# A hybrid decoder layer on one core: the output projection of the first token half with channels on the partitions

## The chip, the cores and the metric

The kernel runs on one core of a Trainium2 chip. The metric is device time in microseconds (us). Before the change the median of three runs is 2372.8 us (2372.53 to 2372.96).

## The reference, cut to what matters

One layer over 1024 tokens and 2048 channels in float32: an RMS norm, one wide input projection, two recurrent mixers (mLSTM and HGRN2), and then the tail, which is all that the change touches:

```python
y = jnp.concatenate([y_a, y_b], axis=-1)                       # (1, 1024, 2048)
h = h + jnp.einsum('bsc,cd->bsd', y, w_out)                    # output projection, residual
e = jnp.einsum('bsr,rd->bsd', p, w_pe)                         # 256 -> 2048
gate = jax.nn.sigmoid(jnp.einsum('bsd,de->bse', rmsnorm(h, pe_norm_w), w_pg))
h = h + gate * e
out = rmsnorm(h, final_norm_w)                                 # over the channels of a token
```

## The kernel before, in words

The tokens are worked in two halves of 512 (`half` 0 and 1). First both halves go through the input projection and the mixers; the mixers leave `y` with channels on the 128 partitions and tokens along the row, in device memory (`y_dram`, 16 pieces a half). Then the tail runs for half 0 and for half 1.

Every float32 operand of a large matmul is split into a high and a low part (`split`, lines 119 and 120: a cast on ScalarE, a subtraction on VectorE), and `mm3` (lines 253 to 255) makes three matmuls of each product. Weights come as pieces of 128x1024, loaded and split three pieces ahead (`next_piece`, `load_piece`).

The tail of a half, before: the sixteen `y` pieces are loaded (`yr`, three staging buffers, line 692) and split into `ys`, tiles of the pool `upool`. `upool` has 17 buffers under one tag, and all of these use it: the inputs `u` of the projections, `ys`, and the results `h2`, two blocks of 128x512 in one tile. Four column blocks `cb` of the output projection follow. In each, the stationary operand is a 128-token slice of `ys` and the moving one is 512 weight columns, so that a result `ps[t]` has 128 tokens on the partitions and 512 channels in the row. VectorE adds the residual (`ht`, line 720), ScalarE squares it into a sum per token (line 722), `h` goes to memory, and TensorE transposes the four 128x128 blocks of each of four channel groups (`pht`, line 729), because the next matmul contracts over the channels. From the transposed block come the two parts of `hn` (lines 732, 733). In the gate's four blocks, ScalarE takes the sigmoid straight from the result with the norm of the token as a per-partition scale (line 785), VectorE multiplies by `pe`, adds `h` and the final norm's weight (lines 786, 792, 797). After the last block the norm `r3` of each token is a scalar per partition: eight tiles of a half are scaled on ScalarE (line 809), eight on VectorE (lines 805, 807), and all are written out (line 810).

The order of the work is not written by hand: a list scheduler plays the program on a timing model and fixes the order on each engine, earlier instructions of the program first among those that are ready; buffers of one tag are handed to tiles by the pool. The engines then keep that order on the chip. Work of different stages is interleaved: the first column blocks of half 0's output projection run while the last HGRN2 unit of half 1 is still at work. The pool `tl`, which holds `pp`, `hn` and the small tiles of the tail, lies where the mixers' tiles were.

Lines that the steps touch:

```python
692  nc.sync.dma_start(out=yr, in_=y_dram[half][k])
720  nc.vector.tensor_tensor(out=ht, in0=ps[t], in1=xr, op=ALU.add)
729  nc.tensor.transpose(pt[:, t * P:(t + 1) * P], hts[t][:, j * P:(j + 1) * P], ident)
788  h2t = upool.tile([P, 2, HT], F32, tag="u", name=f"h2_{half}_{cb}_{t}")
809  nc.scalar.activation(out=ho, in_=ho, func=AF.Copy, scale=r3)
```

Of the kernel before, what the change touches and what calls it, by code (L numbers as in the profile page):

```python
# [16 lines left out]
F32 = mybir.dt.float32  # L17
F32R = mybir.dt.float32r
BF16 = mybir.dt.bfloat16
U32 = mybir.dt.uint32  # L20
AF = mybir.ActivationFunctionType
ALU = mybir.AluOpType
AX = mybir.AxisListType

P = 128
S = 1024
D = 2048
KT = D // P
HT = 512
NC = HT // P  # L30
# [8 lines left out]
HOLD = 2  # L39
LATE = [f"bg1_3_{pc}" for pc in (1, 3, 5, 7)]  # L40

V_NORM, V_PEN, V_MLN, V_HGN, V_LB, V_CW, V_CB, V_END = 0, 16, 32, 40, 48, 64, 96, 104


@with_exitstack
def hybrid_layer(ctx: ExitStack, tc, x, xT, pT, w_blk, w_v0, w_vw, w_out, w_pg, w_pe, vec, gb, fnw,
                 ident_in, causal_in, lmask_in, out):
    nc = tc.nc
# [3 lines left out]
    upool = ctx.enter_context(tc.tile_pool(name="upool", bufs=17))  # L52
# [13 lines left out]
    def psj(name):  # L66
        return pj.tile([P, 512], F32, tag="pj", name=name)
# [5 lines left out]
    vec_sb = const.tile([P, V_END], F32, name="vec_sb")  # L73
# [3 lines left out]
    ident = const.tile([P, P], F32, name="ident")  # L77
# [5 lines left out]
    ones = const.tile([P, P], F32, name="ones")  # L83
# [27 lines left out]
    state_c = [None] * 4  # L111
    state_s = [None] * 8

    y_dram = [[tc.dram_tile([P, HT], F32, name=f"y_{h}_{k}") for k in range(KT)] for h in range(2)]
    h_dram = [tc.dram_tile([P, D], F32, name=f"h_{t}") for t in range(8)]


    def split(dst_hi, dst_lo, src):
        nc.scalar.copy(out=dst_hi, in_=src)  # L119
        nc.vector.tensor_tensor(out=dst_lo, in0=src, in1=dst_hi.bitcast(F32), op=ALU.subtract)  # L120
# [9 lines left out]
    for half in range(2):  # L130
        for b in range(32):
# [4 lines left out]
            for pc in range(4):  # L136
                if b - 4 in WIDE:
                    continue
                src = w_v0 if b == 2 else w_blk[b]
# [33 lines left out]
    def load_piece(name):  # L173

        while len(w_tiles) < len(w_order) and (len(w_tiles) < AHEAD or w_order[len(w_tiles) - AHEAD][0] != name):
            next_piece()
        return dict(w_tiles[-AHEAD - 4:])[name]
# [494 lines left out]
    for half in range(2):  # L672
# [5 lines left out]
        if half == 1:  # L678
            mlctx.close()
            xh = ctx.enter_context(tc.tile_pool(name="xh", bufs=4, side="right", reuse_waits="tile"))  # L680
# [4 lines left out]


    tl = ctx.enter_context(tc.tile_pool(name="tl", bufs=1, reuse_waits="tile"))
    for half in range(2):
        ys = []
        for k in range(KT):  # L690
# [5 lines left out]
        pp = tl.tile([P, 2, 2 * HT], F32R, tag="pp", bufs=1, name=f"pp{half}")  # L696
        for kk in range(2):
            pr_ = stage.tile([P, HT], F32, tag="xs", name=f"praw{half}_{kk}")
            nc.sync.dma_start(out=pr_, in_=pT[:, kk, half * HT:(half + 1) * HT])
            split(pp[:, 0, kk * HT:(kk + 1) * HT], pp[:, 1, kk * HT:(kk + 1) * HT], pr_)  # L700
        hns = [None] * KT
        ss = small.tile([P, NC, 4], F32, tag="ssx", name=f"ss2_{half}")
        for cb in range(4):
            ps = [psj(f"po{half}_{cb}_{t}") for t in range(NC)]
            for pc in range(8):
                hl = load_piece(f"o{half}_{cb}_{pc}")
                for kk in range(2):
                    k = pc * 2 + kk
                    for t in range(NC):
                        ts = slice(t * P, (t + 1) * P)  # L710
                        sl = slice(kk * 512, (kk + 1) * 512)
                        mm3(ps[t], ys[k][:, 0, ts], ys[k][:, 1, ts], hl[:, 0, sl], hl[:, 1, sl], k == 0, k == KT - 1)
            hts = []
            for t in range(NC):
                tt = half * NC + t
                cs = slice(cb * 512, (cb + 1) * 512)
                xr = xh.tile([P, 512], F32, tag="xr", name=f"xr{half}_{cb}_{t}")
                nc.sync.dma_start(out=xr, in_=x[tt * P:(tt + 1) * P, cs])
                ht = xh.tile([P, 512], F32, tag="ht", name=f"ht{half}_{cb}_{t}")
# [5 lines left out]
            for j in range(4):  # L725
                k = cb * 4 + j
                pt = psm(f"pht{half}_{k}")
                for t in range(NC):
                    nc.tensor.transpose(pt[:, t * P:(t + 1) * P], hts[t][:, j * P:(j + 1) * P], ident)
                hn = tl.tile([P, 2, HT], F32R, tag="hn2", bufs=16, name=f"hnt{half}_{k}")  # L730
                pw = vec_sb[:, V_PEN + k:V_PEN + k + 1]
                nc.scalar.activation(out=hn[:, 0], in_=pt, func=AF.Copy, scale=pw)
                nc.vector.scalar_tensor_tensor(out=hn[:, 1], in0=pt, scalar=pw, in1=hn[:, 0].bitcast(F32),
                                               op0=ALU.mult, op1=ALU.subtract)
# [6 lines left out]
        h2 = [[None] * 4 for t in range(NC)]  # L741
# [78 lines left out]
def _layout(inp):  # L820
    f = np.float32
    x = np.ascontiguousarray(np.asarray(inp["x"])[0])
    w = np.asarray(inp["w_in"])[0]
    cols = []
    for h in range(4):
        cols.append([(h * 128, 128), (512 + h * 128, 128)])
        cols.append([(2048 + h * 256, 256)])
        cols.append([(1024 + h * 256, 256)])
        cols.append([(3072 + h * 256, 256)])
    for p in range(4):  # L830
        q, fg, i, g = 4104 + p * 256, 5128 + p * 256, 6152 + p * 256, 7176 + p * 256
        cols.append([(i, 256)])
        cols.append([(q, 128), (fg, 128)])
        cols.append([(q + 128, 128), (fg + 128, 128)])
        cols.append([(g, 256)])
    v0 = np.empty((P, KT, 264), f)
    v0[:, :, 0:256] = w[:, 1024:1280].reshape(KT, P, 256).transpose(1, 0, 2)
    v0[:, :, 256:264] = w[:, 4096:4104].reshape(KT, P, 8).transpose(1, 0, 2)
    blk = np.empty((32, P, KT, 256), f)
    for b, cs in enumerate(cols):  # L840
        o = 0
        for c, n in cs:
            blk[b, :, :, o:o + n] = w[:, c:c + n].reshape(KT, P, n).transpose(1, 0, 2)
            o += n
    vw = np.empty((3, P, KT, 512), f)
    for i, b in enumerate(WIDE):
        vw[i, :, :, 0:256] = blk[b]
        vw[i, :, :, 256:512] = blk[b + 4]

    def blocks(m, kt):  # L850
        return np.ascontiguousarray(np.asarray(m)[0].reshape(kt, P, 4, 512).transpose(2, 1, 0, 3))

    vec = np.empty((P, V_END), f)
    vec[:, V_NORM:V_NORM + 16] = np.asarray(inp["norm_w"])[0].reshape(16, P).T
    vec[:, V_PEN:V_PEN + 16] = np.asarray(inp["pe_norm_w"])[0].reshape(16, P).T
    vec[:, V_MLN:V_MLN + 8] = np.asarray(inp["ml_norm_w"])[0].reshape(8, P).T
    vec[:, V_HGN:V_HGN + 8] = np.asarray(inp["hg_norm_w"])[0].reshape(8, P).T
    vec[:, V_LB:V_LB + 16] = np.asarray(inp["hg_lb"]).reshape(16, P).T
    vec[:, V_CW:V_CW + 32] = np.asarray(inp["conv_w"])[0].reshape(4, 8, P).transpose(2, 1, 0).reshape(P, 32)
    vec[:, V_CB:V_CB + 8] = np.asarray(inp["conv_b"])[0].reshape(8, P).T  # L860
    gb = np.stack([np.asarray(inp["ml_b_i"])[0], np.asarray(inp["ml_b_f"])[0]], axis=1)

    ident = np.eye(P, dtype=f)
    jj, tt = np.meshgrid(np.arange(P), np.arange(P), indexing="ij")
    causal = np.where(jj <= tt, 0.0, -BIG).astype(f)
    lm = np.zeros((P, NMASK, 64), np.uint32)
    j = np.arange(P)[:, None]
    c = np.arange(64)
    lm[:, 0] = j == 2 * c
    lm[:, 1] = j == c // 2 * 4  # L870
    lm[:, 2] = j == c // 2 * 4 + 1
    for li, s in enumerate(LEVELS):
        t = (c // s) * 2 * s + s + c % s
        lm[:, 3 + li] = (j // (2 * s) == t // (2 * s)) & ((j // s) % 2 == 0)
    return {
        "x": x, "xT": np.ascontiguousarray(x.T),
        "pT": np.ascontiguousarray(np.asarray(inp["p"])[0, 0].T.reshape(2, P, S).transpose(1, 0, 2)),
        "w_blk": blk, "w_v0": v0, "w_vw": vw, "w_out": blocks(inp["w_out"], KT), "w_pg": blocks(inp["w_pg"], KT),
        "w_pe": blocks(inp["w_pe"], 2), "vec": vec, "gb": np.ascontiguousarray(gb),
        "fnw": np.ascontiguousarray(np.asarray(inp["final_norm_w"]).reshape(1, D)),  # L880
        "ident": ident, "causal": causal, "lmask": lm,
    }
# [16 lines left out]
```

## Time and profile before

| | |
|---|---|
| median of 3 runs | 2372.8 us (2372.53 to 2372.96) |
| the profiled execution's own time | 2372.51 us |
| its span in the trace | 2370.5 us |
| TensorE (PE) busy | 2355.8 us, 99% of the span |
| VectorE (DVE) busy | 1170.9 us, 49% |
| ScalarE (ACT) busy | 765.8 us, 32% |
| granted TensorE clock, mean | 0.999 |

Busy time is the time in which at least one instruction of the engine runs. Matmuls overlap in the pipeline: one of 512 columns is shown 0.39 us long, but the next starts 0.227 us after it, so starts, not lengths, give its cost. "PE" is the matmul, "PEld" the weight load, "SPq" the queue that issues most DMAs.

### The profile page before, as it was taken

The numbers are of one execution on the slowest core, as the hardware profiler recorded it, in microseconds if no ns is written. First come the engines' busy times: TensorE is split into PE (matmuls) and PEld (weight loads), VectorE is DVE, ScalarE is ACT, GpSimd is POOL, SyncE is SP. The second block draws the span as 40 slices with busy tenths as digits, with TensorE's granted clock in tenths as the row PEclk, the third lists the DMA queues.
The fourth block names the chain that finished last, engine by engine and source line by source line (L and its number), as shares of the span: only waits on it lengthen the run. The fifth ranks groups of instructions, "written<-read, shape, count | busy, mean of one in ns | idle before, by whom it ended". The sixth has DMA issues, their size and how long they took to land.

```text
span 2370.5 us, 28577 instructions
## 1 busy us (share of the span) xinstructions
PE 2355.8 (99%) x11548; PEld 1984.1 (84%) x11548; DVE 1170.9 (49%) x1657; ACT 765.8 (32%) x1211; POOL 66.3 (3%) x96
## 2 busy tenths in 40 slices
PE   9999999999999999999999999999999999999998
PEld 7898888888888898988888888888888888888887
DVE  6655254265556857343534563675433444333336
ACT  6433232222222434232322222241423334332235
POOL 0000000000000000000000000000000000000000
PEclk9999999999999999999999999999999999999999
DMA  8433332322222423333333222343444456444436
GB/s 322 140 99 107 97 101 87 107 82 88 83 96 90 151 72 116 92 113 98 99 115 98 80 82 88 89 147 125 138 125 133 133 157 221 140 153 134 120 117 217
DMA packets 93452, 287.42 MB, mean 121 GB/s; under 512 B 10872, under 2 KB 11640, under 8 KB 93320
## 3 DMA queue, kind: packets, MB, share of 16 engines
q1 hardware_dynamic: 88200, 268.82, 36.5%
q0 software_dynamic: 5120, 16.78, 1.8%
q8 instruction: 90, 1.47, 0.3%
q14 instruction: 42, 0.34, 0.0%
HBM read 260.36 MB, written 25.20 MB: 120 GB/s over the span
## 4 chain that ended last, share of the span: by engine, by line
PE 99%; DMA 0%; DVE 0%; SPq 0%; ACT 0%; issue 0%; ACTq 0%; POOLq 0%
PE pj L254 15%; PE pj L253 15%; PE pj L255 15%; PE pt L253 5%; PE pt L255 5%; PE pt L254 5%; PE po L253 5%; PE pg L253 5%; PE po L255 5%; PE pg L254 5%; PE po L254 5%; PE pg L255 5%; PE pl L594 2%; PE pe L255 1%; PE pe L254 1%; PE pe L253 1%
## 5 line engine op out<-in xcount | busy, mean ns | idle before, releaser
L253 PE MATMUL pj<-u,hl 128*128 128x512 f32 x1536 | 603.5, 394 | 5.3 <-ACT hl L119 5.3
L254 PE MATMUL pj<-u,hl 128*128 128x512 f32 x1536 | 602.4, 392 | 0.1
L255 PE MATMUL pj<-u,hl 128*128 128x512 f32 x1536 | 601.2, 392 | 0.0
L120 DVE TENSOR_TENSOR hl<-raw,hl 128x1024 fp32r<-128x1024 f32 (+2 forms) x259 | 313.7, 1212 | 449.2 <-ACT hl L119 448.4
L119 ACT CAST hl<-raw 128x1024 fp32r<-128x1024 f32 (+2 forms) x259 | 269.4, 1040 | 819.8 <-PE pj L255 554.1
L253 PEld LDWEIGHTS pj<-u,hl 128*128 128x128 f32 x1536 | 288.8, 188 | 64.8 <-ACT hl L119 5.3
L254 PEld LDWEIGHTS pj<-u,hl 128*128 128x128 f32 x1536 | 289.1, 188 | 59.9 <-DVE u L241 0.9
L255 PEld LDWEIGHTS pj<-u,hl 128*128 128x128 f32 x1536 | 289.0, 188 | 59.6 <-issue 0.2
L254 PE MATMUL pt<-hl,u 128*128 128x512 f32 (+2 forms) x640 | 223.7, 350 | 0.0
L253 PE MATMUL pt<-hl,u 128*128 128x512 f32 (+2 forms) x640 | 222.9, 349 | 0.5 <-DVE raw L385 0.5
L255 PE MATMUL pt<-hl,u 128*128 128x512 f32 (+2 forms) x640 | 221.9, 348 | 0.0
L253 PE MATMUL po<-hl_o,ys 128*128 128x512 f32 x512 | 200.5, 393 | 0.0
L254 PE MATMUL po<-hl_o,ys 128*128 128x512 f32 x512 | 200.0, 391 | 0.0
L255 PE MATMUL po<-hl_o,ys 128*128 128x512 f32 x512 | 199.4, 390 | 0.0
L253 PE MATMUL pg<-hl_g,hnt 128*128 128x512 f32 x448 | 174.9, 390 | 0.0
L254 PE MATMUL pg<-hl_g,hnt 128*128 128x512 f32 x448 | 174.5, 390 | 0.0
L255 PE MATMUL pg<-hl_g,hnt 128*128 128x512 f32 x448 | 174.3, 389 | 0.0
L120 DVE TENSOR_TENSOR hl_o<-raw_o,hl_o 128x1024 fp32r<-128x1024 f32 x64 | 78.4, 1225 | 153.9 <-ACT hl_o L119 153.9
L120 DVE TENSOR_TENSOR hl_g<-raw_g,hl_g 128x1024 fp32r<-128x1024 f32 x56 | 68.6, 1225 | 167.4 <-ACT hl_g L119 167.4
L253 PEld LDWEIGHTS pt<-hl,u 128*128 128x128 f32 x640 | 120.6, 189 | 15.7 <-issue 0.8
L254 PEld LDWEIGHTS pt<-hl,u 128*128 128x128 f32 x640 | 120.8, 189 | 14.9 <-issue 0.2
L255 PEld LDWEIGHTS pt<-hl,u 128*128 128x128 f32 x640 | 120.5, 189 | 15.0 <-issue 0.2
(263 smaller groups left out, 2638.4 us busy)
## 6 DMA issues: line engine op xcount, KB each, us to landing
raw<-in_w_blk_dram SPq DMA_DIRECT2D x199, 512.0 KB, 3.9
raw_o<-in_w_out_dram SPq DMA_DIRECT2D x64, 512.0 KB, 3.7
raw_g<-in_w_pg_dram SPq DMA_DIRECT2D x56, 512.0 KB, 3.7
raw<-in_w_vw_dram SPq DMA_DIRECT2D x48, 512.0 KB, 3.6
yr<-y SPq DMA_DIRECT2D x32, 256.0 KB, 4.2
xr<-in_x_dram SPq DMA_DIRECT2D x32, 256.0 KB, 5.7
h<-ht POOLq DMA_DIRECT2D x32, 256.0 KB, 6.2
hr<-h SPq DMA_DIRECT2D x32, 256.0 KB, 3.7
```

Source lines behind the costliest of these rows:

```text
L119: nc.scalar.copy(out=dst_hi, in_=src)
L120: nc.vector.tensor_tensor(out=dst_lo, in0=src, in1=dst_hi.bitcast(F32), op=ALU.subtract)
L253: nc.tensor.matmul(ps, lhsT=ah, rhs=bh, start=first, stop=False)
L254: nc.tensor.matmul(ps, lhsT=ah, rhs=bl, start=False, stop=False)
L255: nc.tensor.matmul(ps, lhsT=al, rhs=bh, start=False, stop=last)
L594: nc.tensor.matmul(pl[0:M, c * 64:(c + 1) * 64], lhsT=kf[:, c * P:c * P + M], rhs=qv[:, c * nb:(c + 1) * nb, 1, :], start=True, stop=True)
```

## The change

Half 0's tail becomes a function of its own, `rows_first`; half 1's stays. In it the weight slice is stationary and 512 tokens of `ys` move, so that every result has 128 channels on the partitions and the half's 512 tokens in the row. The residual comes from the transposed input `xT`, `h` is kept transposed, and `hn` is made from `ht` directly. The sums of squares over the channels go over partitions: blocks are squared and added up elementwise in `acc`, and `row_rstd` sums `acc` with matmuls against ones, takes the power, and spreads the result over the partitions with a matmul against a diagonal. `rb` is then a 128x512 factor that VectorE multiplies in. The final weight is a scalar per partition (sixteen more columns in `vec`). `h2` tiles hold blocks `k` and `k+1`. The output of half 0 is written transposed into the first half of the output buffer, and the host puts it back.

```diff
+    def row_rstd(acc, n, name):
+        pc = psm(f"pc{name}")
+        for t in range(NC):
+            nc.tensor.matmul(pc[:, t:t + 1], lhsT=acc[:, t * P:(t + 1) * P], rhs=ones[:, 0:1], start=True, stop=True)
+        r = rstd_of(pc[:, 0:NC], n, NC, f"rr{name}", tag="rstdx")
+        dg = xh.tile([P, 512], F32, tag="xr", name=f"dg{name}")
+        nc.vector.tensor_tensor(out=dg.rearrange("p (c t) -> p c t", t=P),
+                                in0=ident.unsqueeze(1).broadcast_to([P, NC, P]),
+                                in1=r.unsqueeze(2).broadcast_to([P, NC, P]), op=ALU.mult)
+        pb = psm(f"prow_{name}")
+        nc.tensor.matmul(pb, lhsT=ones, rhs=dg, start=True, stop=True)
+        rb = tl.tile([P, HT], F32, tag="rb2", bufs=1, name=f"rb_{name}")
+        nc.vector.tensor_copy(out=rb, in_=pb)
+        return rb
+
+    def add_square(acc, k, dst, src):
+        nc.scalar.activation(out=acc if k == 0 else dst, in_=src, func=AF.Square)
+        if k > 0:
+            nc.vector.tensor_tensor(out=acc, in0=acc, in1=dst, op=ALU.add)
+
+    def rows_first(ys, pp):
+        acc = tl.tile([P, HT], F32, tag="fb", bufs=1, name="acc2")
+        ...
+                        mm3(ps[j], hl[:, 0, sl], hl[:, 1, sl], ys[k][:, 0], ys[k][:, 1], k == 0, k == KT - 1)
+            for j in range(4):
+                k = cb * 4 + j
+                xr = xh.tile([P, 512], F32, tag="xr", name=f"xr0_{k}")
+                nc.sync.dma_start(out=xr, in_=xT[k * P:(k + 1) * P, 0:HT])
+                ht = xh.tile([P, 512], F32, tag="ht", name=f"ht0_{k}")
+                nc.vector.tensor_tensor(out=ht, in0=ps[j], in1=xr, op=ALU.add)
+                nc.gpsimd.dma_start(out=hT_dram[k], in_=ht)
+                hn = tl.tile([P, 2, HT], F32R, tag="hn2", bufs=16, name=f"hnt0_{k}")
+                pw = vec_sb[:, V_PEN + k:V_PEN + k + 1]
+                nc.scalar.activation(out=hn[:, 0], in_=ht, func=AF.Copy, scale=pw)
+                nc.vector.scalar_tensor_tensor(out=hn[:, 1], in0=ht, scalar=pw, in1=hn[:, 0].bitcast(F32),
+                                               op0=ALU.mult, op1=ALU.subtract)
+                hns.append(hn)
+                add_square(acc, k, xr, ht)
+        ...
+            extra(0)
+            extra(1)
+            ps = [psj(f"pg0_{cb}_{j}") for j in range(4)]
+            ...
+                if cb == 0 and pc == 2:
+                    rb = row_rstd(acc, D, "x2")
+                    acc3 = tl.tile([P, HT], F32, tag="fb", bufs=1, name="acc3")
+                if pc == 4:
+                    extra(2)
+                    extra(3)
+            for j in range(4):
+                k = cb * 4 + j
+                hr = xh.tile([P, 512], F32, tag="xr", name=f"hr0_{k}")
+                nc.sync.dma_start(out=hr, in_=hT_dram[k])
+                gt = xh.tile([P, 512], F32, tag="ht", name=f"gt0_{k}")
+                nc.vector.tensor_tensor(out=gt, in0=ps[j], in1=rb, op=ALU.mult)
+                nc.scalar.activation(out=gt, in_=gt, func=AF.Sigmoid)
+                nc.vector.tensor_tensor(out=gt, in0=pes[j], in1=gt, op=ALU.mult)
+                if k % 2 == 0:
+                    h2t = upool.tile([P, 2, HT], F32, tag="u", name=f"h2_0_{k}")
+                hh = h2t[:, k % 2]
+                nc.vector.tensor_tensor(out=hh, in0=gt, in1=hr, op=ALU.add)
+                add_square(acc3, k, hr, hh)
+                h2.append(hh)
+        rb = row_rstd(acc3, D, "x3")
+        for k in range(KT):
+            nc.vector.scalar_tensor_tensor(out=h2[k], in0=h2[k], scalar=vec_sb[:, V_FN + k:V_FN + k + 1], in1=rb,
+                                           op0=ALU.mult, op1=ALU.mult)
+            nc.sync.dma_start(out=outT[k * P:(k + 1) * P, :], in_=h2[k])
+
     for half in range(2):
         ...
+        if half == 0:
+            rows_first(ys, pp)
+            continue
```

`extra(j)` makes the projection of `p` for channel block `j`, as `pe` was made before.

## Rows read from the trace of the kernel before

**Rows 1.** The page: busy time, and the chain that ended last, by engine.
```profile
PE 2355.8 (99%) x11548; PEld 1984.1 (84%) x11548; DVE 1170.9 (49%) x1657; ACT 765.8 (32%) x1211; POOL 66.3 (3%) x96
...
PE 99%; DMA 0%; DVE 0%; SPq 0%; ACT 0%; issue 0%; ACTq 0%; POOLq 0%
```

**Rows 2.** Waits of TensorE over the whole span: total us, times, longest.
```profile
PE pj L253 <- ACT hl L119: 5.3, 1, 5.3
```

**Rows 3.** Chain in order of time (start us, us): the transposes of one column block.
```profile
1740.39 0.44 PE pht L729 x4
...
1744.28 0.87 PE pht L729 x8
```

**Rows 4.** Timeline of TensorE: a float32 spreading matmul (two records) among ordinary ones.
```profile
50.98 0.40 PE L253 MATMUL pj<-u,hl 128*128 128x512 f32 x1
51.21 1.02 PE L204 MATMUL rb<-dgx,ones 128*128 128x512 f32 x2
...
52.30 0.40 PE L255 MATMUL pj<-u,hl 128*128 128x512 f32 x1
```

**Rows 5.** Chain in order of time: float32 matmuls of 64 columns, two records each.
```profile
1639.68 1.33 PE pl L594 x16
...
1648.60 1.07 PE pl L594 x16
```

**Rows 6.** Timeline of SyncE's queue: loads of half 1's first y pieces.
```profile
1685.42 0.92 SPq L692 DMA_DIRECT2D yr<-y  x2
```

**Rows 7.** Timelines of ScalarE and VectorE as the last h2 tiles of half 0 are written.
```profile
1937.48 1.65 ACT L119 CAST ys<-yr 128x512 fp32r<-128x512 f32 x3
...
1936.94 0.68 DVE L792 TENSOR_TENSOR h<-gt,hr 128x512 f32<-128x512 f32 x1
...
1939.28 0.69 DVE L792 TENSOR_TENSOR h<-gt,hr 128x512 f32<-128x512 f32 x1
```

**Rows 8.** Timelines of TensorE and ScalarE where half 0's gate ends.
```profile
1983.33 0.39 PE L253 MATMUL po<-hl_o,ys 128*128 128x512 f32 x1
...
1981.49 2.73 ACT L785 ACTIVATE gt<-pg,r 128x512 f32<-128x512 f32 x4 [2.35 <-PE pg L255]
...
1989.31 3.79 ACT L809 ACTIVATE h<-h,r 128x512 f32<-128x512 f32 x6
1993.00 1.03 ACT L119 CAST hl_o<-raw_o 128x1024 fp32r<-128x1024 f32 x1
1994.20 0.62 ACT L119 CAST ys<-yr 128x512 fp32r<-128x512 f32 x1 [0.17 <-DMA out_dram<-h]
```

**Rows 9.** Tile yr from 1500 us on: y pieces cast, subtracted, loaded (ns min/median/max).
```profile
L119 ACT CAST ys<-yr x31: 604/620/623, 1561.8 to 2013.2; 128x512 fp32r<-128x512 f32 x31
L120 DVE TENSOR_TENSOR ys<-yr,ys x31: 681/689/696, 1562.9 to 2013.8; 128x512 fp32r<-128x512 f32 x31
...
DMA to landing us min/median/max: 2.4/4.2/7.4
```

**Rows 10.** Groups by form, 1500 us to the end: busy us, mean ns.
```profile
L733 DVE SCALAR_TENSOR_TENSOR hnt<-pht,vec_sb,hnt 128x512 fp32r<-128x512 f32 x32 | 21.9, 745 | 20.3 <-ACT hnt L732 20.3
...
L729 PE MATMUL pht<-ident,ht 128*128 128x128 f32 x128 | 18.0, 272 | 0.0
...
L125 POOL TENSOR_TENSOR r<-r,neghalf 128x4 f32<-128x4 f32 x2 | 2.1, 1035 | 3.0 <-DVE r L124 3.0
```

**Rows 11.** Timeline of TensorE at the start of the program.
```profile
5.26 1.22 PE L253 MATMUL pj<-u,hl 128*128 128x512 f32 x2 [5.26 <-ACT hl L119]
...
10.80 0.74 PE L253 MATMUL pj<-u,hl 128*128 128x512 f32 x2
```

**Rows 12.** Timeline of ScalarE: first write into pool tl, at the mixers' end.
```profile
1682.44 1.14 ACT L119 CAST pp<-praw 128x512 fp32r<-128x512 f32 x2
```

**Rows 13.** Busy time by stretch: PE, PEld, DVE, ACT, POOL, granted clock, DMA.
```profile
6.00:10.00 4.00, 4.00 (x11) 3.13 (x10) 2.25 (x9) 1.73 (x4) 0.00 (x0) 1.00 0.84 284
...
1786.00:1983.00 197.00, 197.00 (x878) 163.17 (x876) 76.12 (x90) 64.04 (x92) 2.11 (x3) 1.00 0.45 139
```

More of the change, by code (lines that the diff above doesn't have):

```diff
@@ L40 @@
 LATE = [f"bg1_3_{pc}" for pc in (1, 3, 5, 7)]
-V_NORM, V_PEN, V_MLN, V_HGN, V_LB, V_CW, V_CB, V_END = 0, 16, 32, 40, 48, 64, 96, 104
+V_NORM, V_PEN, V_MLN, V_HGN, V_LB, V_CW, V_CB, V_FN, V_END = 0, 16, 32, 40, 48, 64, 96, 104, 120
 @with_exitstack
@@ L112, in hybrid_layer @@
     state_s = [None] * 8
+    outT = out[0:HT, :].rearrange("t d -> (t d)").rearrange("(c t) -> c t", t=HT)
     y_dram = [[tc.dram_tile([P, HT], F32, name=f"y_{h}_{k}") for k in range(KT)] for h in range(2)]
     h_dram = [tc.dram_tile([P, D], F32, name=f"h_{t}") for t in range(8)]
+    hT_dram = [tc.dram_tile([P, HT], F32, name=f"hT_{k}") for k in range(KT)]
     def split(dst_hi, dst_lo, src):
@@ new lines, in add_square, with extra @@
+    def add_square(acc, k, dst, src):
[4 more added lines that the diff above has]
+        acc = tl.tile([P, HT], F32, tag="fb", bufs=1, name="acc2")
+        hns = []
+        for cb in range(4):
+            ps = [psj(f"po0_{cb}_{j}") for j in range(4)]
+            for pc in range(8):
+                hl = load_piece(f"o0_{cb}_{pc}")
+                for kk in range(2):
+                    k = pc * 2 + kk
+                    for j in range(4):
+                        sl = slice(kk * 512 + j * P, kk * 512 + (j + 1) * P)
+                        mm3(ps[j], hl[:, 0, sl], hl[:, 1, sl], ys[k][:, 0], ys[k][:, 1], k == 0, k == KT - 1)
[13 more added lines that the diff above has]
+                add_square(acc, k, xr, ht)
+        h2 = []
+        acc3 = None
+        for cb in range(4):
+            wpe = load_piece(f"e0_{cb}")
+            pes = [None] * 4
+            def extra(j):
+                pes[j] = psm(f"pe0_{cb}_{j}")
+                for kk in range(2):
+                    sl = slice(kk * 512 + j * P, kk * 512 + (j + 1) * P)
+                    ts = slice(kk * HT, (kk + 1) * HT)
+                    mm3(pes[j], wpe[:, 0, sl], wpe[:, 1, sl], pp[:, 0, ts], pp[:, 1, ts], kk == 0, kk == 1)
+            extra(0)
+            extra(1)
+            ps = [psj(f"pg0_{cb}_{j}") for j in range(4)]
+            for pc in range(8):
+                hl = load_piece(f"g0_{cb}_{pc}")
+                for kk in range(2):
+                    k = pc * 2 + kk
+                    for j in range(4):
+                        sl = slice(kk * 512 + j * P, kk * 512 + (j + 1) * P)
+                        mm3(ps[j], hl[:, 0, sl], hl[:, 1, sl], hns[k][:, 0], hns[k][:, 1], k == 0, k == KT - 1)
+                if cb == 0 and pc == 2:
[4 more added lines that the diff above has]
+                    extra(3)
+            for j in range(4):
+                k = cb * 4 + j
[16 more added lines that the diff above has]
+            nc.sync.dma_start(out=outT[k * P:(k + 1) * P, :], in_=h2[k])
@@ L860, in _layout @@
     vec[:, V_CB:V_CB + 8] = np.asarray(inp["conv_b"])[0].reshape(8, P).T
+    vec[:, V_FN:V_FN + 16] = np.asarray(inp["final_norm_w"]).reshape(16, P).T
     gb = np.stack([np.asarray(inp["ml_b_i"])[0], np.asarray(inp["ml_b_f"])[0]], axis=1)
@@ L897 @@
     r = _run(nc, [arrays], core_ids=[0])
-    return r.results[0]["out_0_dram"].reshape(1, S, D)
+    o = np.asarray(r.results[0]["out_0_dram"]).reshape(S, D)
+    return np.concatenate([o[:HT].reshape(D, HT).T, o[HT:]])[None]
```

## The prediction

> **What bounds the kernel now.** I read the page first: TensorE is busy for 2355.8 of 2370.5 us, and the chain of waits is TensorE in 99% of its length [rows 1]. A busy matmul engine can still wait, so the list of waits came next: TensorE's one wait of size in the whole program is 5.3 us before the first matmul [rows 2]. So the time is the sum of TensorE's start spacings plus a start and an end. An edit counts if it takes work off TensorE, puts work on it, or makes it wait; what only VectorE or ScalarE do is hidden while TensorE has its operands. In half 0's gate stage VectorE is busy for 76 of 197 us and ScalarE for 64 [rows 13].
>
> All sums are made against the profiled execution's own 2372.5 us (span 2370.5 and 2.0 around it), 0.3 below the median, 2372.8.
>
> **Taken off TensorE.** The large matmuls keep count and shape (128x128 against 512). Half 0's 64 transposes go. In the chain of one block, 16 of them stand as two groups of four (0.44 us each, one is shown) and one of eight (0.87) [rows 3]: 1.75 us, so 4 x 1.75 = 7.0 us. Gain: 7.0.
>
> **Put on TensorE.** `row_rstd` runs twice. Its spreading matmul is the float32 form that the first norm uses: the ordinary matmul before it starts at 50.98, the second one behind it at 52.30, 1.32 us with two ordinary spacings of 0.227 in it, so it costs 0.87 us [rows 4]. Its four one-column sums are not in the trace; the nearest are float32 matmuls of 64 columns, 16 records in 1.07 to 1.33 us [rows 5], 0.067 to 0.083 a record. Eight records make 0.5 to 0.7; four ordinary spacings, 0.9, are the bound above. I take 0.7. Together 2 x (0.87 + 0.7) = 3.1 us (2.7 to 3.5). If nothing waits, the change is worth 7.0 - 3.1 = 3.9 us.
>
> **Hidden in the blocks.** VectorE gains 30 additions into `acc`, 16 products with `rb` and 16 closing instructions, at 0.69 to 0.75 us [rows 7, 10], and loses half 0's weight products and its share of the scaling: about 30 us more over the 300 us of half 0's tail, under TensorE's 384 or 408 matmuls per block. What it delays at a block's end is the freeing of the fourth result: VectorE takes it only after the squares and sums of the blocks before it, some 5 us after the block's last matmul. TensorE has the other three results free by then and 18 matmuls of them per weight piece (4.1 us), with two or three pieces at hand, so I cost this at 0; without that cover it is 2 to 3 us a boundary, eight boundaries. The residual's buffer `xr` now also takes the square and comes free later. That matters once: the pool `tl` was first written at 1682.4, when the mixers had ended [rows 12], so block 0's `hn` and `acc` wait for that, and three of block 1's `xr` loads with them, landing near 1693 to 1696 by 4 to 7 us a load [rows 9], 1 to 3 us late for their additions. Again the results that are free cover it; bounds 0 and 3, taken 0. SyncE's and GpSimd's queues get the same number of residual loads, `h` stores and output stores, and lose four loads of the final weight.
>
> **Where half 0's tail meets half 1's.** This is where I expect the time to go. Half 1's projection needs `ys` of half 1, in the order k = 0 to 15, twelve matmuls each (12 x 0.227 = 2.72 us). In the kernel before, three `y` pieces could be staged long ahead, from 1685 on [rows 6]; the buffers of `upool` were free when the fourth output block ended, near 1786, as only four `h2` tiles were taken until the third gate block. Yet the first cast into `ys` runs at 1937.48, within the 2.3 us between the third and the fourth of that block's `h2` sums, 1936.94 and 1939.28 [rows 7]. The fourth writes the last `h2` tile. I read from it that buffers of one tag are given out in program order: `ys` of half 1 can't pass an `h2` tile that hasn't been given out. Before, that point came 45.9 us ahead of the gate's end (1983.33 [rows 8]). With the change the eighth tile belongs to k = 14 and 15, in the last block, and is first written by the third block's sum, behind the gate's end.
>
> The step in order of time, T = 0 at the gate's last matmul:
> - The first result is free for VectorE at -1.8 (the sigmoids began at 1981.49 [rows 8]). Its chain is now product, sigmoid, product, sum, square, sum, four times: 16 VectorE instructions, some 0.6 apart where independent and 0.7 in the last chain. The eighth tile's sum comes near 4.5, the last sum near 10.
> - `ys` 0 is cast at 4.5 to 5.1 and subtracted in the first gap, near 6.4: TensorE's first wait, 6.4 us. `ys` 1 and 2 follow by 8.7 and 10, as gaps allow. The buffers that they free are loaded again in some 4.2 us [rows 9], so pieces 3 and 4 are split by 14.6, while VectorE waits for the norm.
> - The norm: column sums to 11, VectorE 0.15 and GpSimd 1.04 [rows 10] with their handovers to 12.4, the diagonal to 13.1, spreading to 14.1, copy to 14.8.
> - Then sixteen closing products are ready at once, earlier in the program than any split of half 1. That such work goes first is shown by ScalarE's six scalings at 1989.31, behind which the weight cast stood until 1993.00 [rows 8]. They are 0.745 us each [rows 10], 0.66 apart: 10.7 us, until 25.5. Piece 5 is subtracted by 26.2.
> - Until 26.2 TensorE has had five k (13.6 us) and the second norm's matmuls (1.6, already counted). It waited 26.2 - 13.6 - 1.6 = 11.0 us.
>
> Bounds: 0 if `ys` comes as early as before; 26.2 - 8.2 - 1.6 = 16.4 if only the three staged pieces get through before the closing products. I take 11.0, the sum by the rows. Behind it, pieces 6 to 15 arrive faster than TensorE uses them (three in some 6.5 us against 8.2), so nothing more is late.
>
> After a wait TensorE may restart slowly. It waited 5.26 us at the start and then took from 5.26 to 10.80 for twelve matmuls [rows 11], 0.46 each instead of 0.227: 2.8 us lost. That is near the lower of its two levels, 1.2 GHz, though the granted clock is 1.00 in that stretch [rows 13]. Of the two waits here (6.4 and 4.6 us), the first one's slow start falls inside the second wait; the second costs 0 to 2.8. The start's wait is the nearest row: 2.8.
>
> The Trainium skill ("TensorE: Matmul & The Clock Gate", section "What's actually happening") speaks against the change here: throttled is TensorE's default and activity releases it, so that a wait can cost more than its length. By that rule the term of 2.8 stands; without it the sum is 2.8 lower. The start of this trace agrees in its spacings, not in its granted clock.
>
> **Sum:** 2372.5 - 7.0 + 3.1 + 11.0 + 2.8 = 2382.4; on the median's footing 2382.7, rounded to 2382. Slower by about 9 us.
>
> **Rivals.**
> 1. *The splits keep their lead* (not slower). If a free buffer goes to whoever is ready, `ys` 0 to 8 are split during the gate as before, k = 9 is needed at 9 x 2.72 + 1.6 = 26.1 and subtracted by about 27: a wait of 0 to 2. Then -3.9 + 1 gives 2370, between 2368.6 and 2371. For it: nothing in the code orders the two. Against it: the idle buffers from 1786 to 1937 [rows 7]. It decides from whether a cast into `ys` of half 1 runs before the last gate block ends.
> 2. *Only the staged pieces get through.* If VectorE's gaps in the closing chain aren't used, three k are done before the closing products: wait 16.4, sum 2372.5 - 3.9 + 16.4 + 2.8 = 2387.8, and up to 3 more from block boundaries: 2388 to 2391.
> 3. *The transposes cost more than their spacing.* Their busy time is 18.0 us for 128 [rows 10], 9.0 for 64 if it all counts; with 2.7 added and no wait, -6.3: 2366. Their spacings [rows 3] speak against it. This is also the best that the change could do.
>
> **How the numbers follow.** A measurement tells about 0.2% (4.7 us) from no change: below 2368.1 is faster, above 2377.5 slower. The forecast (2376 to 2387): 0.50. Rival 1: 0.23, nearly all within 0.2%. Rival 2: 0.18, slower. Rival 3: 0.09, faster. Of the forecast's cases 0.04 fall below 2377.5; of rival 1's, 0.01 below 2368.1. So faster 0.10, same 0.26, slower 0.64. The range from 2368 to 2390 leaves out rival 3 and the end of rival 2; the forecast's own range is 2376 to 2387.
>
> **What would show it.** Right: no cast into half 1's `ys` before the last gate block's third sum; TensorE waiting on `ys` around half 1's first output block, twice, 11 us in all; sixteen closing products in a row on VectorE; 64 fewer transposes; slow spacings after a wait. Wrong: casts into `ys` during the gate, or TensorE without a wait there; then the time is near 2369. Waits on VectorE's `ht` or `gt` at every block boundary would show that the cover in the blocks was misjudged.

## The result, and the profile after

The changed kernel takes 2387.8 us, the median of four runs (2386.5 to 2388.8), against 2372.9 beside it: ratio 1.0063, 95% interval 1.0048 to 1.0078. It is 15.0 us slower. The direction and the place were forecast; the size (2382) was not, and the largest part of the miss is a cost that no step of the prediction held.

The page after, the lines that answer to [rows 1], and the list of TensorE's waits that answers to [rows 2] (total us, times, longest):

```profile
PE 2364.5 (99%) x11504; PEld 1983.1 (83%) x11504; DVE 1198.8 (50%) x1694; ACT 757.2 (32%) x1171; POOL 64.6 (3%) x93
...
PE 98%; DVE 1%; DMA 0%; ACT 0%; issue 0%; SPq 0%; ACTq 0%; POOLq 0%
```
```profile
PE pj L255 <- ACT hl L121: 5.6, 1, 5.6
PE po L255 <- ACT ys L121: 3.7, 1, 3.7
PE po L257 <- DVE ys L122: 2.5, 1, 2.5
```

There are two new waits of TensorE, both on `ys`, 6.2 us together, and 1% of the chain now lies on VectorE. But TensorE's busy time, too, is 8.7 us longer, with 44 fewer records of it. Waits can't do that, and the slower matmuls behind them (below) make up only half of it: matmuls elsewhere take longer, too.

The chain in order of time through the seam, where half 0's tail meets half 1's (start us, us), shows what stands between the two halves:

```profile
1979.87 1.39 DVE gt L772 x2
1981.28 0.63 ACT gt L773
1981.98 1.05 ACT hl_o L121
1983.05 0.68 DVE gt L774
1983.73 0.61 DVE h L778
1984.36 0.63 ACT hr L707
1984.99 0.52 ACT ys L121
1985.55 0.80 PE po L255
1986.35 0.43 PE po L256
...
2005.25 0.87 PE prow_x L701 x2
2006.15 0.70 DVE rb_x L703
...
2014.84 2.73 DVE h L783 x4
2017.56 1.14 DVE hl_o L122
2018.70 0.61 DVE ys L122
2019.35 2.07 PE po L257 x4
2021.43 0.43 PE po L255
```

First the end of half 0's gate, up to the first cast into half 1's `ys`; then the norm and the closing products (L783), and behind them a weight piece and the next `ys`. After each wait the matmuls start 0.43 us apart. ScalarE's timeline has the first cast, VectorE's the closing products in a row; the last line has TensorE's busy time and granted clock behind the first wait:

```profile
1984.90 1.65 ACT L121 CAST ys<-yr 128x512 fp32r<-128x512 f32 x3
```
```profile
2006.87 10.69 DVE L783 SCALAR_TENSOR_TENSOR h<-h,vec_sb,rb_x 128x512 f32<-128x512 f32 x16
```
```profile
1985.50:1991.50 6.00, 5.95 (x14) 4.38 (x15) 5.97 (x10) 2.93 (x5) 0.00 (x0) 0.50 0.53 150
```

Where the time went, from the starts of TensorE's matmuls in each trace (us; counted from the first matmul to the last; one execution of each kernel; "gate's end" is one spacing behind its last start). The rows below "after" are runs that the next section describes:

| kernel | before `po` of half 0 | `po`, half 0 | gate, half 0 | gate's end to half 1's first `pht` | the rest |
|---|---|---|---|---|---|
| before | 1582.5 | 198.2 | 197.4 | 43.5 | 334.4 |
| after | 1584.0 | 195.3 | 196.8 | 56.3 | 339.1 |
| after, buffers 256 bytes on | 1583.1 | 195.1 | 195.0 | 57.6 | 334.4 |
| after, pairs | 1583.7 | 195.3 | 196.8 | 56.5 | 339.2 |
| after, pairs and `hn2` buffers | 1584.5 | 195.3 | 196.8 | 46.3 | 340.2 |
| the same, buffers 1024 bytes on | 1583.4 | 195.1 | 195.0 | 46.3 | 334.4 |
| the same, 64 transposes put back | 1582.5 | 198.2 | 199.2 | 46.3 | 334.7 |

The first column differs by up to 2.0 us between these executions, whose programs are alike there but for the places of their tiles, and is not argued from. The seam (the fourth column) lost 12.8 us. But the last column is half 1's own tail, whose code the change doesn't touch, and it lost 4.7. There the matmuls are the same and start farther apart. VectorE, ScalarE and the waits say nothing of it; the windows do. Each line is TensorE over 190 gate matmuls in a row of half 1 (window, length, busy, granted clock, DMA), in the kernel before and in the one after:

```profile
2222.48:2265.32 42.84, 42.84 (x190) 1.00 0.36 107
```
```profile
2235.19:2279.29 44.10, 44.10 (x190) 1.00 0.34 103
```

42.84 / 189 is 0.2267 us a start, 44.10 / 189 is 0.2333, at the same clock and with no more DMA. What has changed for half 1 is where its tiles lie: `vec_sb` grew from 104 to 120 columns, 64 bytes a partition, and every buffer allocated behind it on that side (`hn2`, `pp`, the mixers' tiles) moved.

### The profile page after: what moved, and what is told of

It reads as the page before. It is cut to its first block, busy times and chain, and to the rows that moved or that the text cites. A ratio compares the mean times of both kernels' runs of the same rounds, so it can differ in the third digit from the quotient of the medians.

```text
span 2386.2 us, 28488 instructions
## 1 busy us (share of the span) xinstructions
PE 2364.5 (99%) x11504; PEld 1983.1 (83%) x11504; DVE 1198.8 (50%) x1694; ACT 757.2 (32%) x1171; POOL 64.6 (3%) x93
## 4 chain that ended last, share of the span: by engine, by line
PE 98%; DVE 1%; DMA 0%; ACT 0%; issue 0%; SPq 0%; ACTq 0%; POOLq 0%
PE pj L256 15%; PE pj L255 15%; PE pj L257 15%; PE pt L255 5%; PE pt L257 5%; PE pt L256 5%; PE pg L257 5%; PE pg L255 5%; PE pg L256 5%; PE po L257 5%; PE po L255 5%; PE po L256 5%; PE pl L596 2%; PE pe L257 1%; PE pe L255 1%; PE pe L256 1%
## 5 line engine op out<-in xcount | busy, mean ns | idle before, releaser
L121 ACT CAST hl_o<-raw_o 128x1024 fp32r<-128x1024 f32 x64 | 67.0, 1048 | 188.7 <-PE po L257 153.6
L121 ACT CAST hl_g<-raw_g 128x1024 fp32r<-128x1024 f32 x56 | 58.7, 1048 | 184.5 <-PE pg L257 151.0
L255 PE MATMUL po<-hl_o,ys 128*128 128x512 f32 x256 | 102.4, 400 | 3.7 <-ACT ys L121 3.7
L257 PE MATMUL po<-hl_o,ys 128*128 128x512 f32 x256 | 99.4, 399 | 2.5 <-DVE ys L122 2.5
L256 PE MATMUL po<-hl_o,ys 128*128 128x512 f32 x256 | 101.2, 395 | 0.0
L255 PE MATMUL po<-ys,hl_o 128*128 128x512 f32 x256 | 100.1, 392 | 0.0
```

Of the source, the lines that this page charges most:

```text
L255: nc.tensor.matmul(ps, lhsT=ah, rhs=bh, start=first, stop=False)
L256: nc.tensor.matmul(ps, lhsT=ah, rhs=bl, start=False, stop=False)
L257: nc.tensor.matmul(ps, lhsT=al, rhs=bh, start=False, stop=last)
```

## Experiments

**Is it the place of the tiles?** The kernel before, with nothing but the wider tile:

```diff
-    vec_sb = const.tile([P, V_END], F32, name="vec_sb")
+    vec_sb = const.tile([P, 120], F32, name="vec_sb")[:, 0:V_END]
```

> The kernel before, with 16 unused columns behind vec_sb, so that every later buffer moves by 64 bytes as it does in the kernel after. Theory 'addresses': in the kernel after the matmuls that read hn2, pp and the column sums' tiles start 0.2333 to 0.2339 us apart where these tiles are the stationary operand and 0.2290 where they are the moving one, against 0.2266 to 0.2273 before, because the 64 bytes moved the tiles. Then both halves here show 0.2333 to 0.2339 in their gates: (2 x 864 + 80) x 0.0066 = +12 us, 2385 us. Rival 'company': the wider spacing comes from what the other engines do beside the matmuls in the kernel after; then 0 us, 2373 us.

Measured: 2384.7 us, ratio 1.0049 (1.0036 to 1.0061). 16 columns that nobody reads cost the old kernel 11.7 us. The same window as above shows the after kernel's spacing, which settles it against "company":

```profile
2231.73:2275.83 44.10, 44.10 (x190) 1.00 0.35 103
```

The kernel after, with the tile widened once more:

```diff
-    vec_sb = const.tile([P, V_END], F32, name="vec_sb")
+    vec_sb = const.tile([P, 136], F32, name="vec_sb")[:, 0:V_END]
```

> The kernel after, with 16 unused columns more, so that later buffers lie 128 bytes from where they were in the kernel before. Theory 'addresses': the spacings go back to 0.2266 to 0.2273 us in half 1's gate and the column sums and to 0.2270 in half 0's gate: (864 + 80) x 0.0066 + 864 x 0.0020 = -8 us, 2380 us. Rival 'company': no change, 2388 us.

Measured: 2389.6 us, 1.0071 (1.0059 to 1.0084): no gain, so the expectation failed. The spacing in half 1 went to 43.92 / 189 = 0.2324, and in half 0's gate, where `hn` moves, up from 0.2290 to 0.2320 (medians). So 128 bytes are no better than 64; the tiles are not indifferent to the place, but its period is longer than I had taken.

```profile
2238.62:2282.54 43.92, 43.92 (x190) 1.00 0.34 103
```

By a map of the addresses, which no run here shows, `u`, `ys`, the weights' tiles, `ones_r`, `hn2` and `pp` all lie at 128 modulo 256 bytes in the kernel before. What the runs show is what a move from there costs. So the next pair asked for the period, and whether the place or the difference of the two operands counts. The kernel before with `const.tile([P, 168], ...)` in the line above:

> The kernel before, with 64 unused columns behind vec_sb: later buffers move by 256 bytes. A move by 64 bytes cost 11.7 us and spacings of 0.2333 to 0.2338 us; in the kernel after, a further 64 (128 in all) left them at 0.2320. Theory 'period of 256': a tile's place counts modulo 256 bytes, 0.2270 us, 2373 us. Rival 'longer period' (512 or 1024 bytes): spacings between 0.2290 and 0.2340, 2376 to 2385 us.

Measured: 2373.4 us, 1.0001 (0.9992 to 1.0010). A move by 256 bytes costs nothing. And the kernel before with everything moved by 64:

```diff
+    pre = ctx.enter_context(tc.tile_pool(name="pre", bufs=1))
+    nc.vector.memset(pre.tile([P, 16], F32, name="pre"), 0.0)
     upool = ctx.enter_context(tc.tile_pool(name="upool", bufs=17))
```

> The kernel before, with an unused tile of 64 bytes ahead of every pool of the left side, so that u, ys, the weights' tiles and ones_r move by 64 bytes together with hn2, pp and vec_sb. Theory 'difference': what counts is how the two operands of one matmul lie to each other; all spacings stay at 0.2266 to 0.2273 us, 2373 us. Rival 'place': what counts is where a tile lies; then the projections, too, go from 0.2270 to some 0.2335 us: 7700 matmuls of 512 columns by 0.0066, +50 us, 2420 us or more.

Measured: 2373.3 us, 0.9999 (0.9990 to 1.0008), and the gate's spacing 0.2267. All operands moved by 64 bytes together cost nothing; it is the difference that counts. Sorted by the stationary tile's address less the moving one's, modulo 256 bytes, with the kernel before as 0 by that map: 0 gives 0.2267, 64 gives 0.2333, 128 gives 0.2320 to 0.2324, 192 (half 0's gate after the change) gives 0.2290.

So the kernel after was given `const.tile([P, 168], ...)`, too:

> The kernel after, with later buffers 256 bytes from where they were in the kernel before and nothing else. Theory 'difference modulo 256 bytes': all spacings are 0.2266 to 0.2273 us again, both TensorE waits (3.65 and 2.5 us) and both stretches at the lower clock stay: (864 + 80) x 0.0066 + 864 x 0.0020 = -8 us, 2380 us, near the 2382 that was forecast without the addresses. If the waits grow as the matmuls get faster, 2382 to 2384.

Measured: 2378.7 us, 1.0025 (1.0014 to 1.0036), 9.1 below the kernel after. Half 0's gate and half 1's tail are back (the table's third row), and both waits are still there:

```profile
PE po L255 <- ACT ys L121: 3.7, 1, 3.7
PE po L257 <- DVE ys L122: 3.3, 2, 2.6
```

This is the change without the shifted buffers: 5.6 us slower than the kernel before, not 15. Its profiled execution took 2381.3 us, 2.6 above the median, and the eight range from 2377.8 (mean granted clock 0.998) to 2381.6 (0.996); so its row of the table stands for one of the longer ones.

**Is it the hand-out of `upool`'s buffers?** Tiles `k` and `k+8` share a buffer, closing in the order 0, 8, 1, 9, ...:

```diff
-                if k % 2 == 0:
-                    h2t = upool.tile([P, 2, HT], F32, tag="u", name=f"h2_0_{k}")
-                hh = h2t[:, k % 2]
+                if k < 8:
+                    h2t.append(upool.tile([P, 2, HT], F32, tag="u", name=f"h2_0_{k}"))
+                hh = h2t[k % 8][:, k // 8]
```

> The kernel after, with half 0's gate tiles k and k+8 in one buffer instead of k and k+1, so that the eighth buffer is given out at k = 7 (second gate block) and not at k = 14 (fourth). Theory 'hand-out': half 1's ys are split in half 0's gate, both TensorE waits behind its end (3.65 and 2.5 us) go, and with them the two stretches at the lower clock (6.8 and 3.4 us): -11 us, 2377 us. Rival 'closing': the 16 closing products in a row on VectorE still hold up the splits that follow them; only the first wait and its stretch of lower clock go: -7 us, 2381 us. Rival 'loads': SP's queue, with the weights' and hr loads, keeps yr late; under -3 us, 2385 us or more.

Measured: 2387.5 us, 1.0063 (1.0049 to 1.0077): nothing gained. Yet the hand-out theory's first sentence holds: ScalarE's first cast into half 1's `ys` moved from 1984.90 to 1887.59, right behind the second gate block, and the wait behind the gate's end is gone. The two waits that came instead both stand at the tenth piece, 8.1 us together:

```profile
1887.59 1.65 ACT L121 CAST ys<-yr 128x512 fp32r<-128x512 f32 x3
```
```profile
PE po L257 <- DVE ys L122: 6.0, 1, 6.0
...
PE po L255 <- ACT ys L121: 2.1, 1, 2.1
```
```profile
2008.92 0.62 ACT L121 CAST ys<-yr 128x512 fp32r<-128x512 f32 x1 [3.13 <-DMA out_dram<-h]
```
```profile
2005.24 10.69 DVE L783 SCALAR_TENSOR_TENSOR h<-h,vec_sb,rb_x 128x512 f32<-128x512 f32 x16
2015.85 1.22 DVE L122 TENSOR_TENSOR hl_o<-raw_o,hl_o 128x1024 fp32r<-128x1024 f32 x1
2016.98 1.89 DVE L122 TENSOR_TENSOR ys<-yr,ys 128x512 fp32r<-128x512 f32 x3
```

Seventeen buffers less eight for `h2` leave nine `ys`. TensorE had those nine early, ran through them while the norm and the closing products were still going, and stood at the tenth: first for its cast, at 2008.92, when an output tile had left, then for its subtraction, which came only behind all sixteen products, at 2016.98. Only the second of these had slow matmuls behind it, one such stretch where the kernel after has two, so the time came out the same. Starting earlier only moved the wait. Both edits at once, the pairs and the 136 columns:

> Both edits in one: gate tiles k and k+8 in one buffer, and 16 unused columns more behind vec_sb. If both theories hold and their parts add, -19 us against the kernel after, 2369 us, 4 us below the kernel before: what the 64 transposes are worth (7.0) less the two spreading steps (3.1). If only 'hand-out' holds 2377, if only 'addresses' 2380, if neither 2388.

Measured: 2389.8 us, 1.0071 (1.0058 to 1.0083). Neither edit pays: 128 bytes is a bad place and the pairs alone move the wait. So `ys` needs more buffers that don't come from the closing tiles. Half 0's `hn2` tiles come free in its last gate block, and half 1 needs them all only when `ys` is done with:

```diff
-            y = upool.tile([P, 2, HT], F32R, tag="u", name=f"ys{half}_{k}")
+            if half == 1 and 9 <= k < 13:
+                y = tl.tile([P, 2, HT], F32R, tag="hn2", bufs=16, name=f"ys{half}_{k}")
+            else:
+                y = upool.tile([P, 2, HT], F32R, tag="u", name=f"ys{half}_{k}")
```

> The paired kernel, with half 1's ys 9 to 12 in buffers of hn2, which half 0's gate has given up, and not in those of the closing products' tiles. In the paired kernel the first wait went and a longer one came: ys9, 6.0 us, behind the 16 closing products, in all 8.1 us of waits and 6.8 us at the lower clock, against 6.2 and 10.2 in the kernel after. Theory 'closing': with 13 pieces split before the products (13 x 2.7 = 35 us of TensorE work) nothing waits there: -8.1 -3.4, +1.3 for four ys at an odd place, 2377 us. Rival 'last three': ys13 to ys15 still stand behind the products on VectorE and cost 2 to 4 us of wait and a stretch of lower clock, 2380 to 2383 us.

Measured: 2379.0 us, 1.0023 (1.0014 to 1.0033), 8.8 below the kernel after. No wait on `ys` is left in the list, and the clock stays at 1.00 through the seam, which shrinks from 56.3 to 46.3 us.

The `hn2` buffers (the edit above) without the pairs:

> The kernel after, with half 1's ys 9 to 12 in buffers of hn2 and the gate tiles paired as they were (k and k+1). The hand-out theory says that ys0 still waits for the eighth gate tile: the first wait (3.65 us and 3.4 lost at the lower clock) stays; the second (2.5 and 1.7) needs fewer pieces behind the closing products and goes: -4.2 + 1.3 = -3 us, 2385 us. Rival: pieces 0 to 8 come so late that the second wait only moves, 2387 to 2388 us.

Measured: 2390.3 us, 1.0073 (1.0060 to 1.0085). The rival is right: the first wait stays and the second turns into one on a weight piece, which stands behind the same products on VectorE:

```profile
2009.33 10.68 DVE L783 SCALAR_TENSOR_TENSOR h<-h,vec_sb,rb_x 128x512 f32<-128x512 f32 x16
2019.94 1.21 DVE L122 TENSOR_TENSOR hl_o<-raw_o,hl_o 128x1024 fp32r<-128x1024 f32 x1
```
```profile
2021.20 0.50 PE L256 MATMUL po<-hl_o,ys 128*128 128x512 f32 x1 [2.22 <-DVE hl_o L122]
```

Its profiled execution is the fastest of its five (2387.9, mean granted clock 0.998), so its trace doesn't explain why the median is 2.5 us above the kernel after. The other four show a granted clock of 0.996 to 0.997, so more of their time lay at the lower level; behind which waits, no trace shows.

**Both causes taken away:** pairs, `hn2` buffers and `const.tile([P, 360], ...)`.

> The same, and vec_sb wide enough (360 columns) that later buffers lie 1024 bytes from where they were in the kernel before. If addresses count modulo 1024 bytes or a part of it, every spacing is 0.2266 to 0.2273 us again and -9 us against the run with pairs and hn2 alone: 2368 us, 5 us below the kernel before, which is the transposes' 7.0 less the two spreading steps' 3.1 and what half 0's last block gives. If the period is longer than 1024 bytes, 2376 us.

Measured: 2369.8 us, 0.9985 (0.9976 to 0.9994): 3.6 us faster than the kernel before. The addresses gave 9.2 beyond the pairs and `hn2` buffers. All spacings are at 0.2267 and what is left of the waits at the seam is one of 0.6 us:

```profile
PE po L256 <- DVE hl_o L122: 0.6, 1, 0.6
```

**What are the transposes worth?** They are put back into that kernel, four groups of four behind each of half 0's output blocks.

```diff
+            for j in range(4):
+                pt = psm(f"pht0_{cb * 4 + j}")
+                for t in range(NC):
+                    nc.tensor.transpose(pt[:, t * P:(t + 1) * P], hts[j][:, t * P:(t + 1) * P], ident)
```

> The kernel with pairs, hn2 buffers and 360 columns (2369.8 us), and 64 transposes of ht put back into half 0's output blocks, as many as the change removed; nobody reads what they give. By the spacings, 1.75 us a block or 7.0 us in all: 2376.8 us. By the rival that their busy time counts, 9.0 us: 2378.8 us. If transposes hide behind other work, less than 4 us.

Measured: 2377.2 us, 1.0018 (1.0010 to 1.0027), 7.4 more. By windows over half 0's output projection and gate, without and with them:

```profile
1588.64:1783.71 195.07, 195.07 (x944) 163.39 (x942) 100.60 (x130) 60.94 (x89) 12.62 (x21) 1.00 0.42 137
1783.71:1978.66 194.95, 194.95 (x863) 161.18 (x862) 87.52 (x108) 60.98 (x78) 1.04 (x1) 1.00 0.44 138
```
```profile
1588.28:1786.48 198.20, 198.20 (x983) 166.37 (x982) 98.67 (x126) 58.56 (x86) 11.48 (x19) 1.00 0.42 131
1786.48:1985.69 199.21, 199.21 (x890) 164.71 (x888) 89.87 (x111) 63.45 (x81) 2.12 (x4) 1.00 0.45 139
```

3.1 + 4.3 = 7.4 us.

**Do the mixers' small matmuls feel their place?**

```diff
-        raw = mix.tile([P, 2, HT + 3], F32, tag="raw", bufs=1, name=f"raw{n}")
+        raw = mix.tile([P, 2, HT + 32], F32, tag="raw", bufs=1, name=f"raw{n}")[:, :, 0:HT + 3]
...
-            vt = mix.tile([P, NC, 257], F32, tag="vt", bufs=3, name=f"vt{half}_{b}_{i}")
+            vt = mix.tile([P, 1088], F32, tag="vt", bufs=3, name=f"vt{half}_{b}_{i}")[:, 0:NC * 257].rearrange("p (c v) -> p c v", v=257)
...
-    lb = const.tile([P, 8], F32, name="lb")
+    lb = const.tile([P, 32], F32, name="lb")[:, 0:8]
```

`vec_sb` has 144 columns here; with the 24 of `lb`, later buffers move by 256 bytes.

> The kernel with pairs and hn2 buffers, later buffers 256 bytes on, and padding in the mixers so that qk, vt, S and ident lie at the same place modulo 256 bytes as at, dq and kh (before, they lay 32 to 160 bytes apart). Theory 'every matmul': the mixers' small float32 matmuls (some 150 us of spacings in pl, pn, pu, hpu, hpo) gain up to 3%: 2365 to 2369 us. Rival 'only the long float32r ones': 2370 us, the same as with 360 columns.

Measured: 2370.1 us, 0.9988 (0.9980 to 0.9997), the same as with 360 columns, and no spacing of `pl`, `pn`, `pu`, `hpu` or `hpo` moved. The rival holds: of the matmuls tried, only those of 512 columns and split operands gained. That the padding made the mixers' places equal rests on the map alone.

## Why the prediction was right or wrong

- **TensorE sets the time, the blocks hide the rest: right.** The waits after have nothing at a block boundary, nor at the residual loads near 1690. The "384 or 408 matmuls per block" were misread: half 0's `po` and `pg` are 768 each in four blocks and its `pe` 96, so 192 or 216; no term was worked out from it.
- **Transposes, 7.0: right**, 7.4 by the run that put them back. Rival 3 (9.0) falls.
- **Two norms, 3.1: 3.5,** the bound above. Around the eight column-sum records ordinary starts lie 1.35 us apart with two spacings in it (0.90 for the sums, not 0.7); around the spreading matmul 1.33 (0.87, as in [rows 4]):

```profile
1997.61 0.39 PE L256 MATMUL po<-hl_o,ys 128*128 128x512 f32 x1
1997.83 0.95 PE L694 MATMUL pcx<-ones,acc 128*128 128x1 f32 x8
...
1998.96 0.39 PE L255 MATMUL po<-hl_o,ys 128*128 128x512 f32 x1
...
2004.85 0.40 PE L257 MATMUL po<-hl_o,ys 128*128 128x512 f32 x1
2005.09 1.02 PE L701 MATMUL prow_x<-dgx,ones 128*128 128x512 f32 x2
...
2006.18 0.40 PE L256 MATMUL po<-hl_o,ys 128*128 128x512 f32 x1
```

- **The seam, 11.0 + 2.8: the mechanism right, the size 2.8 too large.** The seam lost 12.8 us, 1.8 of them to the second norm: 11.0 for waits and slow restarts, where 13.8 was forecast. No cast into half 1's `ys` ran before the gate's end, and the run with pairs showed that the hand-out was the reason. But one sign was put too strictly: three casts ran from 1984.90 on, ahead of the last block's third sum (1987.78, first line) and not behind it:

```profile
1987.78 0.68 DVE L778 TENSOR_TENSOR h<-gt,hr 128x512 f32<-128x512 f32 x1
...
1993.09 0.69 DVE L709 TENSOR_TENSOR acc<-acc,hr 128x512 f32<-128x512 f32 x1
...
2001.64 0.69 DVE L697 TENSOR_TENSOR dgx<-ident,rrx 128x512 f32<-128x512 f32 x1 [1.18 <-POOL rrx L127]
```

As before the change (1.8 us, [rows 7]), the casts ran ahead of the sum that first writes the eighth tile, here by 2.9 us; what sets this lead stays open. The first wait was 3.65 us and not 6.4: the cast came 3.2 us behind the gate's end (4.5 was forecast), and the first matmul needed the high half alone, not the subtraction. The second was 2.5 and not 4.6: nine pieces, not five, were subtracted before the closing products, because these began at 2006.87, 25.1 us behind the gate's end, and not at 14.8. The norm's own matmuls stood in TensorE's queue behind half 1's, which was left out of the norm's chain: the column sums (1997.83) began some 4 us behind the end of the last addition into `acc` (second line), the spreading matmul (2005.09) 2.8 behind the end of the diagonal (third line). That is 6.8 of the 10.3 us; the last addition itself was 2 late.
- **The slow restart, 2.8: 4.4.** Both waits had one, here with a granted clock of 0.50, the lower level (1.2 GHz): 14 matmuls 0.43 us apart behind the first and 7 behind the second, 6.15 and 3.04 us for what takes 3.17 and 1.59 at 0.2267. By the trace's record the clock fell within the waits, at 1984.70 and 2018.83, not in the steady stream. The Trainium skill ("TensorE: Matmul & The Clock Gate", section "What's actually happening") says that a throttled clock is the default and that activity releases it. The rows agree: 0.50 behind the first wait, and 1.00 again behind those 14 matmuls. Nor does the start of the trace before speak against it: its record of the clock begins at 10.78 us, where the slow spacings of [rows 11] end, and the 1.00 of [rows 13] ahead of that is only how a stretch without a record is shown.
- **The missing term, 6.7 to 9.1.** That widening `vec` by 16 columns moves all that is allocated behind it was not weighed; the edit was not even costed at nothing. Against the run with later buffers 256 bytes on it cost 9.1 by the medians and 6.7 by the table's second, third and last columns (0.2 + 1.8 + 4.7); the difference stays open, but for what was said of that run's executions. With the terms as the traces have them: 2382.4 + (3.5 - 3.1) - (7.4 - 7.0) - 2.8 + 6.7 = 2386.3. The profiled execution took 2388.1; of the 1.8 left, 1.5 lie in the first column.

So the sum landed 6 us low with errors of opposite sign, and outside its own range (2376 to 2387), though within the wide one. That it came so near is in part luck: what it did weigh came out 4.3 us too slow (9.9 forecast, 5.6 measured with the buffers put back), and that hid part of the missing term. Rival 2 had named 2388, but not for the reason: nine pieces got through, where it had three. Rival 1 falls as it stood; its time, 2370, is what the kernel takes once the splits do keep their lead and the addresses are put back.

## What to carry to other kernels

A wider constant moves every buffer behind it: after such an edit compare the start spacing of matmuls in a stage whose code did not change, before any story about the new code. When a stage's results and the next stage's inputs share a tag, count which request of the one stands in the program ahead of the first request of the other; and when that wait is lifted, count the buffers that are left, since here nine early pieces only moved the wait from the first to the tenth. A norm over the partitions makes all closing work ready at once: a burst of 10.7 us on one engine delays whatever that engine owes the next stage.

## What was not expected of the hardware

Matmuls of 128x128 against 512 columns of split float32 started 0.2267 us apart when the two operands' tiles lay as in the kernel before (at the same place modulo 256 bytes, by the map), and up to 0.2333 apart (2.9%) when one of them had moved against the other by 64, 128 or 192 bytes modulo 256: 11.7 us of 2373 from 64 bytes. Moving both kept 0.2267. Behind waits of 3.65 and 2.54 us the granted clock was 0.50, behind one of 2.22 us (the run with `hn2` buffers alone) it stayed at 1.00. Which part of the engine or memory the 256 bytes belong to was not tried.
